# Four moves at the seam between gating and attention: earlier gated weights, a filler behind the second logits, a fixed order up to the last minimum, exchanged transpose banks

## The chip, the core and the metric

The kernel runs on one core of a Trainium2 chip. The core has engines that run side by side: TensorE (PE in the profile; PEld is its loading of weights) multiplies matrices and transposes, VectorE (DVE) and ScalarE (ACT) read and write both memories on the chip, GpSimd (POOL) works on SBUF only, and SyncE (SP) issues most transfers. TensorE writes to PSUM, eight banks of 512 float32 per partition; SBUF holds the tiles. The metric is the time of one execution on the device in microseconds, the median of several runs.

## The reference

One decoder block on 1024 tokens of width 1024, float32. Eight heads of forgetting attention stand beside a gated branch (gMLP); both go through one output projection, and a gated feed-forward with a causal convolution follows. What matters here:

```
proj = rmsnorm(x) @ w_in                      # q, k, v, u, vg, forget gates
att  = softmax(q k^T / 8 + c_q - c_k, causal) @ v     # 8 heads of 64; c: cumulated log forget gates
mixed = tril(w_s[g]) @ rmsnorm(gelu(vg))[chunk, g] + b_s   # 8 groups, chunks of 128 tokens
sg   = gelu(u) * mixed
h    = x + concat(att, sg) @ w_out
h    = h + conv_ffn(rmsnorm(h))
out  = rmsnorm(h)
```

## The kernel before

Every float32 operand of a matmul is split in a high part (float32r, a rounded copy) and a low part (what is left), and a product is three matmuls: high by high, high by low, low by high. A split is a cast (ACT or POOL) and a subtraction (VectorE or POOL), the second in L166 or L787.

The work comes in stages: the input projections (up to 183 us in the trace), the rest of the v projection (`vmul`, L861, four products of 48 matmuls in sums and differences of halves), the spatial gating (`spatial`, L805 to L815), the transposes of the gated result (`turn_sg`, L831), the attention, then the output projection, the feed-forward and the last norm.

The spatial gating goes over eight groups. For each, TensorE mixes both halves of the tokens into one bank; VectorE forms the gated first half, ACT adds the bias to the second half and POOL multiplies it (L815). `turn_sg(hf, c, ps)` then transposes half `hf` (512 tokens) of column block `c`, four 128x128 transposes into one bank; `sg_hi` (ACT) and `sg_lo` (VectorE) split it into `sgT[c]`. Half 0 uses the banks of tag "s", half 1 those of tag "b".

The gated half of the output projection is not a stage of its own. It is cut into sixteen pieces, the fillers (`sg_out`): each is 12 matmuls for 128 tokens by 512 columns (L1068 to L1070), is evacuated by VectorE, which adds the input x (L1071, tile raw, loaded in L1064), and is stored (L1072). The table `FILLS` says behind which step of the attention a filler is issued; (-1, j) means behind the logits of block j of head 0. A filler's bank has the tag "b", of which there are four, shared with the turns and the value products. Its weights are `whs`: two transfers of 512 KB (`sg_load`, L775, tile raw) and four splits (`sg_split`) into buffers of the tag whl, of which there are four too; the last users before them are the weights of the v products.

The attention of a head takes its eight blocks of 128 queries from the longest (7) to the shortest (0). `logits_mm` (L980, L981) needs one of two places of two banks; `logits_min` (VectorE, L993) adds the mask, takes the row's minimum and moves the logits to SBUF, which frees the place; `logits_exp` (ACT, L1003) follows. Then `turn_p` (L1028) transposes the exponentials, cast and subtraction (L1029, L1030) split them, and `values` (L1044) multiplies by v. The attention's PSUM layout lies over that of the stage before: the first two places cover the four banks of tag "s".

What sets the order: the planner of the language puts each engine's instructions in order, by their place in the program and by its own estimate of when they are ready. `after` adds an order between two instructions without a wait. `seq` chains TensorE's instructions from the v products on as written. While `act.on` and `dve.on` are set, all instructions of ACT and VectorE are chained as written; in the trace their line is then L55. They are set from behind `head_loads(0)` up to the second last part of the gate (`sg_lo(1, 3)`), ahead of the first filler. POOL is not chained. SP issues its transfers one by one; one that must wait holds those behind it. `head_loads(h)` (L878 to L886) loads a head's queries, keys and row sums; the row sums of all heads go through memory (ncr, ncd: L850, L903, L910).

Of the kernel before, what the change touches and what calls it, by code (L numbers as in the profile page):

```python
# [12 lines left out]
ALU = mybir.AluOpType  # L13
AX = mybir.AxisListType
P = 128
# [3 lines left out]
NFF = 22  # L19
WARM = 8  # L20

FILLS = {(-1, j): 1 for j in (5, 3, 2)} | {(h, s): 1 for h in range(6) for s in ((0, 2, 4) if h == 0 else (2, 4))}
FCFG = ("b", 4, 4)


# [38 lines left out]
def after(tc, later, earlier):  # L64
    tc.add_manual_dep(later.ins, earlier.ins.name, mybir.DependencyInfo(
        mybir.DependencyClass.NoSync, mybir.DependencyReason.DATA), reason="order")
# [3 lines left out]
def block_kernel(ctx: ExitStack, tc: tile.TileContext, xT, xtok, wuv, wv0, wva, wvk, wvl, wqk, cpk, bfv,  # L70
# [86 lines left out]
    def split_w(src, hl, hi_eng="act", lo_eng="dve"):  # L157
        h, l = hl
        if hi_eng == "act":
            act.copy(h, src)  # L160
        elif hi_eng == "pool":
            pool.tensor_copy(h, src)
        else:
            dve.tensor_copy(h, src)
        eng = dve if lo_eng == "dve" else pool
        return eng.tensor_tensor(out=l, in0=src, in1=f32(h), op=ALU.subtract)  # L166
# [600 lines left out]

    queued = []

    def sg_load(hf):  # L770

        wrs = []
        for kp in range(2):
            wr = sb("raw", [P, 2, 512])
            queued[:] = [sp.dma_start(out=wr, in_=wos[hf, kp])]  # L775
            after(tc, queued[0], loads[0])
            wrs += [wr[:, 0, :], wr[:, 1, :]]
        return wrs

    splits = []  # L780

    def sg_split(wr, hi="act"):
        w = sb("whl", [P, 2, 512], F32R)
        if hi == "pool":
            x = pool.tensor_copy(w[:, 0], wr)
            after(tc, x, splits[0])
            pool.tensor_tensor(out=w[:, 1], in0=wr, in1=f32(w[:, 0]), op=ALU.subtract)  # L787
        else:
            split_w(wr, (w[:, 0], w[:, 1]), hi, "pool")
        return w  # L790

    def spatial_weights():
# [6 lines left out]
    def spatial():  # L799

        tmp = [sb("pt", [P, 4, 256]) for _ in range(2)]
        for g in range(8):
            ps = bank()
            for hf in range(2):
                m = pe.matmul(ps[:, hf * 256:hf * 256 + 256], ws[:, g, :], vgt[hf][:, :, g * 64:(g + 1) * 64],  # L805
                              start=(hf == 0), stop=(hf == 1), skip_group_check=True)
            v3 = lambda t: t.rearrange("p (t d) -> p t d", d=64)
            u = [ut[hf][:, :, g * 64:(g + 1) * 64] for hf in range(2)]
            dve.scalar_tensor_tensor(out=u[0], in0=v3(ps[:, 0:256]), scalar=bs[:, g:g + 1], in1=u[0],
                                     op0=ALU.add, op1=ALU.mult)  # L810
            t = tmp[g // 4][:, g % 4, :]

            def second():
                act.activation(t, ps[:, 256:512], AF.Identity, bias=bs[:, g:g + 1])
                splits[:] = [pool.tensor_tensor(out=u[1], in0=v3(t), in1=u[1], op=ALU.mult)]  # L815

            if g < 7:
                second()
            if g < 2:
                vlow.append(evac_v(6 + g, 0, vb_[:, (2 + g) * 256:(2 + g) * 256 + 256]))  # L820
            if 1 <= g < 5:
                vlow[g - 1]()
        seq(m)
        return second

    def turn_sg(hf, c, ps):

        if hf == 0:
            sgT[c] = sb("G", [P, 2, 1024], F32R)
        for t in range(4):  # L830
            seq(pe.transpose(ps[:, t * P:(t + 1) * P], ut[hf][:, t, c * P:(c + 1) * P], ident))  # L831
        return ps
# [4 lines left out]
    def sg_hi(hf, c, ps):  # L837
        act.copy(sgT[c][:, 0, sg_o(hf)], ps)
# [35 lines left out]
    def head_loads(h):  # L874
# [11 lines left out]
            loads[h] = sp.dma_start(out=f32(b2s[64:67, hh, :]), in_=ncd[1:4, 1 + h, :])  # L886
        rows[h] = sml.tile([P, 8], F32, tag="rs", name=nm("rs"))

    head_loads(0)
    va_, vb_, vc_ = xy[:, 0], xy[:, 1], xl  # L890
    act.on = dve.on = True
# [6 lines left out]
    vmul(R, vw["S1"], "T1")  # L898
    Q = [sbank() for _ in range(2)]
    vmul(Q, vw["A22"], "T4")  # L900
    whs, wrs = [], sg_load(0)
    for n, s in ((0, 1), (1, 1), (2, 2), (3, 1)):
        after(tc, sp.dma_start(out=ncd[n].rearrange("h (t p) -> (h t) p", p=P), in_=sums[s]), queued[0])  # L903
    for j, o in enumerate(hw):
        dve.tensor_tensor(out=vb_[:, o], in0=R[j], in1=vb_[:, o], op=ALU.subtract)
        dve.tensor_tensor(out=vc_[:, o], in0=va_[:, o], in1=R[j], op=ALU.subtract)
    for m in range(4):
        evac_v(m, 0, vk[:, m, :])()
    sp.dma_start(out=vu[1], in_=vc_.rearrange("p (m c) -> p m c", c=256))
# [1 line left out]
    sp.dma_start(out=f32(b2s[64:67, 0, :]), in_=ncd[1:4, 1, :])  # L911
    V.extend(sb("V", [P, 2, 8, 2, 64], F32R) for _ in range(2))
    vlow = [evac_v(4 + m, 0, vb_[:, m * 256:m * 256 + 256]) for m in range(2)]
    for j, o in enumerate(hw):
        dve.tensor_tensor(out=va_[:, o], in0=va_[:, o], in1=Q[j], op=ALU.add)
    sp.dma_start(out=vu[0], in_=va_.rearrange("p (m c) -> p m c", c=256))
# [1 line left out]
    second = spatial()  # L918
    head_loads(1)

    for c in range(4):
        ps = turn_sg(0, c, sbank())
        sg_hi(0, c, ps)
        sg_lo(0, c, ps)
        if c == 0:
            second()
    for k in range(4):
        whs.append(sg_split(wrs[k], "pool" if k < 2 else "act"))


    attT = [None] * 4
# [124 lines left out]
    def sg_out(whs):  # L1056
        for hf in range(2):
            o = slice(hf * 512, hf * 512 + 512)
            for tt in range(8):
                if hf == 0 and tt == 6:  # L1060
                    nxt = sg_load(1)
                ts_ = slice(tt * P, (tt + 1) * P)
                hs = sb("raw", [P, 512])
                sp.dma_start(out=hs, in_=xtok[ts_, o])  # L1064
                ps = fbank()
                for k in range(4):
                    w = whs[k]
                    seq(pe.matmul(ps, sgT[k][:, 0, ts_], w[:, 0, :], start=(k == 0), stop=False))  # L1068
                    seq(pe.matmul(ps, sgT[k][:, 0, ts_], w[:, 1, :], start=False, stop=False))
                    seq(pe.matmul(ps, sgT[k][:, 1, ts_], w[:, 0, :], start=False, stop=(k == 3)))  # L1070
                dve.tensor_tensor(out=hs, in0=ps, in1=hs, op=ALU.add)  # L1071
                sp.dma_start(out=hpd[tt, :, o], in_=hs)  # L1072
                if hf == 0 and tt == 7:
                    whs = [sg_split(wr) for wr in nxt]
                yield

    filler = sg_out(whs)

    wo = []
# [28 lines left out]
        logits_mm(0, j, firsts[j])  # L1108
    for c in range(4):
        sg_hi(1, c, pts[c])  # L1110
    m7 = logits_min(0, 7, firsts[7])
    sg_lo(1, 0, pts[0])
    sg_lo(1, 1, pts[1])
    m6 = logits_min(0, 6, firsts[6])
    sg_lo(1, 2, pts[2])
    logits_exp(0, 7, m7)
    logits_exp(0, 6, m6)
    logits(0, 5)
    sg_lo(1, 3, pts[3])
    act.on = dve.on = False  # L1120
    act.last = dve.last = None
    fill((-1, 5))
    for j in range(4, -1, -1):
        logits(0, j)
        fill((-1, j))
    due = []
    turned = [turn_p(g) for g in STEPS[0]]
    for n, step in enumerate(STEPS):
# [674 lines left out]
```

## Time and profile before

| | |
|---|---|
| median of 3 runs | 1052.77 us (1052.22 to 1052.96) |
| profiled execution | 1052.88 us |
| its span | 1051.2 us |
| TensorE busy | 1040.2 us, 99% |
| VectorE, ACT, POOL busy | 891.5, 562.6, 217.0 us |
| chain that ended last | PE 96%, DVE 2%, ACT 1% |

All times inside the kernel are microseconds from the start of the span of this one execution. In a row of the timeline stand start, length, engine, line, operation, the tile written and the tiles read by the program's names, shapes and a count; in square brackets how long the engine stood idle before it and what ended that. A row with a count merges several instructions.

### The profile page before, as it was taken

To read this page: it belongs to the slowest core of one execution; us is meant where nothing else is said; L and a number is where in the kernel's file an instruction comes from. 1 tells how busy PE (TensorE), PEld (TensorE's weight loads), DVE (VectorE), ACT (ScalarE), POOL (GpSimd) and SP (SyncE) were. 2 spreads that over 40 slices of the span, in tenths; PEclk is the share of its full clock that TensorE was granted. 3 is DMA by queue.
4 is the path that set the end of the run, shared out by engine and by line. 5 is a ranking of instruction groups with operands and counts; after the bars stand their busy time and mean duration, and the time that the engine had idled before them with its cause. 6 is when DMAs were issued, how large, how long until landed. Compare 5 with 4: busy or idle time off the path is not lost.

```text
span 1051.2 us, 14265 instructions
## 1 busy us (share of the span) xinstructions
PE 1040.2 (99%) x4998; PEld 870.1 (83%) x4998; DVE 891.5 (85%) x1302; ACT 562.6 (54%) x1003; POOL 217.0 (21%) x165
## 2 busy tenths in 40 slices
PE   9999999999999999999999999999999999999997
PEld 7988888978888888888888888888888888888886
DVE  6899887868887779998999999898897866997774
ACT  6776632457876746654344344444444554454654
POOL 0000231320421640243333423323331000000000
PEclk9999999999999999999999999999999999999999
DMA  9722558867755544222255332431322899433432
GB/s 326 235 87 95 154 157 244 227 195 199 209 161 161 158 158 156 80 90 91 80 181 171 120 110 82 131 120 67 129 85 81 305 325 305 117 100 98 142 121 100
DMA packets 67451, 161.66 MB, mean 154 GB/s; under 512 B 8094, under 2 KB 9238, under 8 KB 67380
## 3 DMA queue, kind: packets, MB, share of 16 engines
q1 hardware_dynamic: 67108, 160.72, 47.8%
q8 instruction: 39, 0.64, 0.2%
q14 instruction: 32, 0.26, 0.1%
q10 hardware_dynamic: 272, 0.04, 0.0%
HBM read 115.68 MB, written 45.05 MB: 153 GB/s over the span
## 4 chain that ended last, share of the span: by engine, by line
PE 96%; DVE 2%; ACT 1%; issue 0%; ACTq 0%; DVEq 0%
PE k L1616 20%; PE qc L1356 11%; PE qa L1356 11%; PE qd L1356 11%; PE qb L1356 5%; PE pb L270 5%; PE ps L270 5%; PE pb L1044 3%; PE pb L1028 2%; PE qc L510 2%; PE qd L510 2%; PE qa L510 2%; PE ps L861 2%; PE pl L980 1%; PE pf L1068 1%; PE pl L981 1%
## 5 line engine op out<-in xcount | busy, mean ns | idle before, releaser
L1616 PE MATMUL k<-whb,wha 128*128 128x512 f32 (+1 forms) x936 | 209.9, 386 | 0.0
L1616 PEld LDWEIGHTS k<-whb,wha 128*128 128x128 f32 x936 | 174.1, 188 | 35.8 <-DVE wha L166 0.2
L1356 PE MATMUL qc<-xT,whb 128*128 128x512 f32 x540 | 129.9, 389 | 0.2 <-ACT whb L160 0.2
L1356 PE MATMUL qa<-xB,wha 128*128 128x512 f32 x528 | 127.4, 390 | 0.0
L1356 PEld LDWEIGHTS qc<-xT,whb 128*128 128x128 f32 x540 | 101.3, 188 | 21.6 <-ACT whb L160 0.5
L1356 PEld LDWEIGHTS qa<-xB,wha 128*128 128x128 f32 x528 | 98.8, 188 | 20.8 <-DVE wha L166 0.4
L160 ACT CAST wha<-sg 128x512 fp32r<-128x512 f32 x77 | 47.7, 622 | 96.9 <-PE k L1616 83.5
L160 ACT CAST whb<-sg 128x512 fp32r<-128x512 f32 x82 | 50.5, 617 | 87.0 <-PE qc L1356 67.0
L166 DVE TENSOR_TENSOR wha<-sg,wha 128x512 fp32r<-128x512 f32 x77 | 52.7, 687 | 37.1 <-ACT wha L160 36.9
L1356 PE MATMUL qd<-xB,whb 128*128 128x512 f32 x264 | 63.7, 389 | 0.0
L1356 PE MATMUL qd<-xT,whb 128*128 128x512 f32 x264 | 63.7, 389 | 0.0
L1029 ACT CAST pt<-pb 128x512 fp32r<-128x512 f32 x72 | 40.6, 584 | 38.2 <-PE pb L1028 32.0
L1356 PE MATMUL qb<-xT,whb 128*128 128x512 f32 x252 | 61.0, 389 | 0.0
L166 DVE TENSOR_TENSOR whb<-sg,whb 128x512 fp32r<-128x512 f32 x82 | 57.0, 697 | 4.4 <-ACT whb L160 4.3
L1240 POOL TENSOR_TENSOR sg<-raw 128x512 f32<-128x512 f32 x20 | 30.8, 1541 | 141.1 <-DVE whb L166 80.6
L1356 PEld LDWEIGHTS qd<-xT,whb 128*128 128x128 f32 x264 | 49.5, 188 | 10.5 <-DVE u L1463 0.3
L1356 PEld LDWEIGHTS qd<-xB,whb 128*128 128x128 f32 x264 | 49.5, 188 | 10.3
L1030 DVE TENSOR_TENSOR pt<-pb,pt 128x512 fp32r<-128x512 f32 x72 | 47.3, 685 | 12.2 <-ACT pt L1029 11.9
L1356 PEld LDWEIGHTS qb<-xT,whb 128*128 128x128 f32 x252 | 47.2, 188 | 10.0 <-DVE whb L166 0.3
L1044 PE MATMUL pb<-pt,V 128*128 128x512 f32 (+3 forms) x192 | 49.7, 363 | 0.3 <-DVE pt L1030 0.3
L1243 POOL TENSOR_TENSOR sg<-sg,raw 128x512 f32<-128x512 f32 x20 | 33.0, 1649 | 63.1 <-DVE whb L166 63.1
L1241 POOL TENSOR_TENSOR sg<-sg,raw 128x512 f32<-128x512 f32 x20 | 35.1, 1757 | 47.2 <-issue 44.6
(416 smaller groups left out, 2242.6 us busy)
## 6 DMA issues: line engine op xcount, KB each, us to landing
raw<-wup SPq DMA_DIRECT2D x44, 512.0 KB
sg<-hx SPq DMA_DIRECT2D x77, 256.0 KB
hx<-hs SPq DMA_DIRECT2D x44, 256.0 KB
hx<-ca SPq DMA_DIRECT2D x35, 256.0 KB
xT<-wdn SPq DMA_DIRECT2D x28, 256.0 KB
x<-kd SPq DMA_DIRECT2D x24, 256.0 KB
A<-xtok SPq DMA_DIRECT2D x8, 512.0 KB
raw<-wqk SPq DMA_DIRECT2D x8, 512.0 KB
```

Source lines behind the costliest of these rows:

```text
L160: act.copy(h, src)
L166: return eng.tensor_tensor(out=l, in0=src, in1=f32(h), op=ALU.subtract)
L270: pe.matmul(banks[m], xs(n, xi, k)[:, ms], w[:, wi, :], start=(first and k == 0 and c == 0 and (own or m % 2 == 0)), stop=(k == 3 and c == ...
L510: pe.matmul(ps, w[:, wi, ks], xs(n, xi, k), start=(first and c == 0), stop=(c == 11), skip_group_check=True)
L1029: casts.append(act.copy(pt[:, 0, :], ptr))
L1030: los.append(dve.tensor_tensor(out=pt[:, 1, :], in0=ptr, in1=f32(pt[:, 0, :]), op=ALU.subtract))
L1044: seq(pe.matmul(po[half][:, o:o + w], lhs, pt[:, s, c:c + w], start=(new and s == 0), stop=(s == 1 and (half, k) in ((1, 6), (0, 3))), ski ...
L1240: pool.tensor_tensor(out=s[0], in0=a21, in1=a22, op=ALU.add)
L1241: pool.tensor_tensor(out=s[1], in0=s[0], in1=a11, op=ALU.add)
L1243: pool.tensor_tensor(out=s[3], in0=s[1], in1=a12, op=ALU.add)
L1356: pe.matmul(ps, w[:, wi, ks], xb[:, xi, k, :], start=(first and n == 0), stop=(n == 11), skip_group_check=True)
L1616: pe.matmul((banks[bk + m] if ps is None else ps)[:, o], xh[:, xi, ms], wh[:, wi, o], start=((first and p_ == 0 or new) and n == 0), stop= ...
```

## The change

Four things are edited, all between the v products and the turns of head 0.

1. The gated weights of columns 0 to 511 are loaded ahead of `head_loads(0)` on SP, behind the last store of the projections, and split ahead of the spatial gating: the first two wholly on POOL, the last two with the cast on ACT (inside its fixed order) and the subtraction on POOL. The stores of the row sums are put in order behind the head loads instead of behind the weights.
2. The banks of the transposes of half 0 are allocated together, and the last two allocated are used first.
3. The three fillers among the logits of head 0 stand behind blocks 6, 4 and 2 instead of 5, 3 and 2. The first low part of half 1 moves ahead of the minimum of block 7, since a filler needs a bank.
4. ACT and VectorE stay in the written order up to the minimum and exponential of block 0. A filler's evacuation and store is put off in a list while that holds, and taken from it at written places: the first ahead of the exponential of block 5, the others behind their fillers.

```diff
-FILLS = {(-1, j): 1 for j in (5, 3, 2)} | {(h, s): 1 for h in range(6) for s in ((0, 2, 4) if h == 0 else (2, 4))}
+FILLS = {(-1, j): 1 for j in (6, 4, 2)} | {(h, s): 1 for h in range(6) for s in ((0, 2, 4) if h == 0 else (2, 4))}
...
-    def sg_load(hf):
+    def sg_load(hf, floor=None):
...
-            after(tc, queued[0], loads[0])
+            after(tc, queued[0], floor or loads[0])
...
     def sg_split(wr, hi="act"):
         w = sb("whl", [P, 2, 512], F32R)
-        if hi == "pool":
-            x = pool.tensor_copy(w[:, 0], wr)
-            after(tc, x, splits[0])
-            pool.tensor_tensor(out=w[:, 1], in0=wr, in1=f32(w[:, 0]), op=ALU.subtract)
-        else:
-            split_w(wr, (w[:, 0], w[:, 1]), hi, "pool")
+        split_w(wr, (w[:, 0], w[:, 1]), hi, "pool")
         return w
...
+    whs, wrs = [], sg_load(0, floors["sp"])
     head_loads(0)
...
     vmul(Q, vw["A22"], "T4")
-    whs, wrs = [], sg_load(0)
     for n, s in ((0, 1), (1, 1), (2, 2), (3, 1)):
-        after(tc, sp.dma_start(out=ncd[n].rearrange("h (t p) -> (h t) p", p=P), in_=sums[s]), queued[0])
+        after(tc, sp.dma_start(out=ncd[n].rearrange("h (t p) -> (h t) p", p=P), in_=sums[s]), loads[0])
     for j, o in enumerate(hw):
         dve.tensor_tensor(out=vb_[:, o], in0=R[j], in1=vb_[:, o], op=ALU.subtract)
         dve.tensor_tensor(out=vc_[:, o], in0=va_[:, o], in1=R[j], op=ALU.subtract)
+    for k in range(2):
+        whs.append(sg_split(wrs[k], "pool"))
...
     vlow = [evac_v(4 + m, 0, vb_[:, m * 256:m * 256 + 256]) for m in range(2)]
+    for k in range(2, 4):
+        whs.append(sg_split(wrs[k]))
...
+    pts = [sbank() for _ in range(4)]
+    pts = pts[2:] + pts[:2]
     for c in range(4):
-        ps = turn_sg(0, c, sbank())
+        ps = turn_sg(0, c, pts[c])
         sg_hi(0, c, ps)
         sg_lo(0, c, ps)
         if c == 0:
             second()
-    for k in range(4):
-        whs.append(sg_split(wrs[k], "pool" if k < 2 else "act"))
...
-                dve.tensor_tensor(out=hs, in0=ps, in1=hs, op=ALU.add)
-                sp.dma_start(out=hpd[tt, :, o], in_=hs)
+                def evac(ps=ps, hs=hs, tt=tt, o=o):
+                    dve.tensor_tensor(out=hs, in0=ps, in1=hs, op=ALU.add)
+                    sp.dma_start(out=hpd[tt, :, o], in_=hs)
+
+                if dve.on:
+                    EVAC.append(evac)
+                else:
+                    evac()
...
+    sg_lo(1, 0, pts[0])
     m7 = logits_min(0, 7, firsts[7])
-    sg_lo(1, 0, pts[0])
+    fill((-1, 6))
     sg_lo(1, 1, pts[1])
     m6 = logits_min(0, 6, firsts[6])
     sg_lo(1, 2, pts[2])
     logits_exp(0, 7, m7)
     logits_exp(0, 6, m6)
-    logits(0, 5)
+    m5 = logits_min(0, 5, logits_mm(0, 5, place()))
     sg_lo(1, 3, pts[3])
-    act.on = dve.on = False
-    act.last = dve.last = None
-    fill((-1, 5))
+    EVAC.pop(0)()
+    logits_exp(0, 5, m5)
     for j in range(4, -1, -1):
         logits(0, j)
         fill((-1, j))
+        if EVAC:
+            EVAC.pop(0)()
+    act.on = dve.on = False
+    act.last = dve.last = None
```

More of the change, by code (lines that the diff above doesn't have):

```diff
@@ L775, in sg_load @@
             queued[:] = [sp.dma_start(out=wr, in_=wos[hf, kp])]
-            after(tc, queued[0], loads[0])
+            after(tc, queued[0], floor or loads[0])
             wrs += [wr[:, 0, :], wr[:, 1, :]]
         return wrs
-    splits = []
     def sg_split(wr, hi="act"):
         w = sb("whl", [P, 2, 512], F32R)
-        if hi == "pool":
-            x = pool.tensor_copy(w[:, 0], wr)
-            after(tc, x, splits[0])
-            pool.tensor_tensor(out=w[:, 1], in0=wr, in1=f32(w[:, 0]), op=ALU.subtract)
-        else:
-            split_w(wr, (w[:, 0], w[:, 1]), hi, "pool")
+        split_w(wr, (w[:, 0], w[:, 1]), hi, "pool")
         return w
@@ L814, in second @@
                 act.activation(t, ps[:, 256:512], AF.Identity, bias=bs[:, g:g + 1])
-                splits[:] = [pool.tensor_tensor(out=u[1], in0=v3(t), in1=u[1], op=ALU.mult)]
+                pool.tensor_tensor(out=u[1], in0=v3(t), in1=u[1], op=ALU.mult)
             if g < 7:
@@ L1075, in sg_out @@
                 yield
+    EVAC = []
     filler = sg_out(whs)
```

## Prediction

> **What bounds the kernel now.** I read the page first, then busy time by stretch, then the timeline of each engine around the edited lines.
>
> ```profile
> span 1051.2 us, 14265 instructions
> PE 1040.2 (99%) x4998; PEld 870.1 (83%) x4998; DVE 891.5 (85%) x1302; ACT 562.6 (54%) x1003; POOL 217.0 (21%) x165
> ...
> 207.00:228.00 21.00, 18.87 (x108) 15.64 (x107) 14.27 (x29) 13.76 (x32) 8.35 (x10) 1.00 0.57 163
> 228.00:400.00 172.00, 170.39 (x968) 146.06 (x966) 139.86 (x265) 114.03 (x250) 49.66 (x46) 1.00 0.61 179
> ```
>
> In the last two rows the columns are stretch, its length, busy PE, PEld, DVE, ACT and POOL (instructions in brackets), granted clock, DMA share, GB/s. TensorE sets the end almost everywhere; a change pays only where TensorE stands still. From 207 to 228 us, the stretch that the diff rewrites, it is busy 18.87 of 21 us: 2.13 us idle, the largest hole in the attention. Four rows hold it:
>
> ```profile
> 208.78 1.91 PE L831 MATMUL pb<-ident,A 128*128 128x128 f32 x16
> 211.09 0.50 PE L980 MATMUL pl<-x 128*128 128x512 f32 x1 [0.39 <-DVE G L55]
> 213.86 0.50 PE L980 MATMUL pl<-x 128*128 128x512 f32 x1 [0.74 <-DVE mn L55]
> 214.67 0.39 PE L1068 MATMUL pf<-whl,G 128*128 128x512 f32 x1
> ...
> 217.40 0.39 PE L980 MATMUL pl<-x 128*128 128x512 f32 x1
> ...
> 226.16 0.66 PE L1028 MATMUL pb<-ident,t 128*128 128x128 f32 x4 [0.72 <-DVE raw L1071]
> 227.08 1.25 PE L1028 MATMUL pb<-ident,t 128*128 128x128 f32 x8 [0.27 <-DVE raw L1071]
> 228.28 0.73 PE L1044 MATMUL pb<-pt,V 128*128 128x512 f32 x2
> ```
>
> The reader is to see: the first logits (block 7) wait 0.39 us, after the transposes end at 210.69, for a low part of the gate (G) to leave their PSUM banks; block 5 waits 0.74 us for block 7's minimum (mn); two turns of the exponentials (L1028) wait 0.72 and 0.27 us for a filler's evacuation (raw, L1071). Together 2.12 us. The stretch ends where the first value matmul starts, at 228.28.
>
> The profiled execution took 1052.88 us by its own clock, 1.7 us over its span, and stands 0.11 us above the median 1052.77. A difference under 0.2% (2.1 us) is about what a measurement cannot tell from no change.
>
> **The change part by part.** *Transposes' banks.* The first logits take the PSUM of two of the four gate transposes. Exchanged, those are the two drained first.
>
> ```profile
> 209.15 1.89 DVE L55 TENSOR_TENSOR G<-ps,G 128x512 fp32r<-128x512 f32 x3 [0.16 <-ACT G L55]
> 212.46 1.34 DVE L55 CUSTOM_DVE_ANT_0 t<-pl,t,lim 128x1024 f32<-128x1024 f32 x1 [1.43 <-PE pl L981]
> 213.73 1.28 DVE L55 TENSOR_TENSOR G<-pb,G 128x512 fp32r<-128x512 f32 x2
> 214.93 1.20 DVE L55 CUSTOM_DVE_ANT_0 t<-pl,t,lim 128x896 f32<-128x896 f32 x1
> 216.66 1.07 DVE L55 CUSTOM_DVE_ANT_0 t<-pl,t,lim 128x768 f32<-128x768 f32 x1
> ...
> 218.25 0.94 DVE L993 CUSTOM_DVE_ANT_0 t<-pl,t,lim 128x640 f32<-128x640 f32 x1
> ...
> 225.41 0.69 DVE L1071 TENSOR_TENSOR raw<-pf,raw 128x512 f32<-128x512 f32 x1
> 226.34 1.28 DVE L1071 TENSOR_TENSOR raw<-pf,raw 128x512 f32<-128x512 f32 x2
> 227.54 1.87 DVE L1030 TENSOR_TENSOR pt<-pb,pt 128x512 fp32r<-128x512 f32 x3
> ```
>
> Low parts 1 to 3 run 209.15 to 211.04, 0.63 each, so the second is done by 209.8 and the logits start at 210.69, -0.40. Block 6 needs the last (211.04) and starts near 211.6. Next late would be the transposes themselves.
>
> *First filler behind the second logits.* A filler is 12 matmuls, 214.67 to 217.40, 2.73 us. It now covers block 7's minimum. It needs split weights (next part) and a bank: all four are held by the second transposes, hence the low part moved ahead of the minimum. That part takes 0.64 after 211.04, done 211.7, before block 7's logits end at 212.06 (212.46 less 0.40), so the minimum is not delayed. Block 6 ends at 212.4, then the filler. -0.74.
>
> *Fixed order and deferred evacuations.* Now the three evacuations run at 225.41 to 227.6, behind nearly all minima, and hold three banks. In the new order I lay VectorE out with the rows above (a minimum's row less 0.07 overlap, 0.6 per low part and evacuation): minimum 7 212.06 to 213.3; low part 213.95; minimum 6 215.1; low part 215.7; block 5's logits end at 215.15 + 0.7 + 0.3, so minimum 5 216.1 to 217.1; low part 217.7; evacuation 0 218.3; minimum 4 219.2; evacuation 1 waits for its filler (216.5 + 2.73 + 0.3 = 219.5), 220.1; minima 3 and 2, one step of 0.13 shorter each, 220.9 and 221.5; evacuation 2 waits for 223.0, 223.6; minima 1 and 0, 224.4. Each logits tile needs the minimum two blocks above: block 3 (219.2) that of 5 (217.1), block 2 (219.7) that of 4 (219.2), block 1 (222.7) that of 3 (220.9). None waits; the thinnest margin, 0.5 us, is behind evacuation 0, and past it each microsecond is one of TensorE. Behind each new wait on VectorE (evacuations 1 and 2) stand minima whose logits come after that filler on TensorE anyway. TensorE runs its logits and fillers through to 223.3 (224.8 less 1.13 of waits and some 0.3 of slow first matmuls behind them) and starts the turns there, all four banks empty by 223.6: -0.99. The stores behind the evacuations (L1072) go to SP earlier, in front of nothing that waits.
>
> What is late next is the first turn's cast and subtraction before the first value matmul.
>
> ```profile
> 209.95 1.18 ACT L55 CAST whl<-raw 128x512 fp32r<-128x512 f32 x2
> 210.99 2.09 ACT L55 CAST G<-pb 128x512 fp32r<-128x512 f32 x4
> ...
> 226.04 0.57 ACT L1029 CAST pt<-pb 128x512 fp32r<-128x512 f32 x1
> ```
>
> By TensorE alone (turns from 223.3, 16 transposes at 0.12 by the row of 208.78) the values could start at 225.2. The first cast takes 0.57 and the subtraction 0.65, the latter behind minimum 0 (224.4): done at 225.1 if the cast goes first, 226.6 if it stands behind the last two exponentials. In the row above the cast stands between them; the same here gives 226.0. So the stretch is 2.3 us shorter, between 1.7 and 3.1.
>
> *Gated weights earlier.* Two loads of 512 KB move past the head loads on SP; two POOL casts and two POOL subtractions go ahead of the mixing products, two ACT casts too, with two more POOL subtractions.
>
> ```profile
> 187.58 2.26 SPq L632 DMA_DIRECT2D qd<-G  x2
> ...
> 190.61 0.93 SPq L878 DMA_DIRECT2D x<-qd  x1
> ...
> 194.10 1.00 SPq L775 DMA_DIRECT2D raw<-wos  x2
> ...
> 205.14 0.23 SPq L910 DMA_DIRECT2D x<-ncd  x1
> ...
> 212.29 1.31 SPq L1064 DMA_DIRECT2D raw<-xtok  x3
> 194.00:196.00 2.00, 2.00 (x19) 2.00 (x18) 1.84 (x4) 0.00 (x0) 0.04 (x1) 1.00 0.86 254
> 204.00:206.00 2.00, 2.00 (x11) 1.75 (x10) 2.00 (x5) 0.77 (x3) 1.45 (x2) 1.00 0.17 65
> 193.21 0.29 POOL L851 CAST t<-t 72x128 fp32r<-72x128 f32 x1 [8.38 <-DMA t<-ncr]
> ...
> 202.27 1.60 POOL L815 TENSOR_TENSOR A<-pt,A 128x256 f32<-128x256 f32 x2 [8.22 <-ACT pt L55]
> ...
> 208.72 0.73 POOL L815 TENSOR_TENSOR A<-pt,A 128x256 f32<-128x256 f32 x1 [0.17 <-ACT pt L55]
> 209.39 1.17 POOL L785 CAST whl<-raw 128x512 fp32r<-128x512 f32 x2
> 210.52 2.52 POOL L787 TENSOR_TENSOR whl<-raw,whl 128x512 fp32r<-128x512 f32 x2
> 197.45 0.91 ACT L55 ACTIVATE V<-x,rstd 128x256 fp32r<-128x256 f32 x2 [6.35 <-PE ps L861]
> 201.72 0.47 ACT L55 ACTIVATE pt<-pb,cp 128x256 f32<-128x256 f32 x1 [3.35 <-DVE A L55]
> 194.37 2.80 PE L861 MATMUL ps<-whl,V 128*128 128x256 f32 x22
> ```
>
> The small load ahead (t<-ncr, after the stores at 187.58) is in at 193.2. At 254 GB/s each 512 KB takes 2.1 us, so the weights land at 195.3 and 197.4. The head loads lose 1.00 us of issue and 4.2 us of data; the DMA share falls to 0.17 after 204, so all are in by 204 in either order, and logits want them at 210.7: nothing. The row sums (L910, 205.14) wait for stores behind the same bytes: nothing.
>
> POOL needs 1.17 + 2.52 for the first two: 195.3 to 199.0. ACT is free 198.36 to 201.72. Its first cast (0.59) fits at 198.4; the second writes a buffer that the last V product reads (48 matmuls from 194.37, 0.12 each: 200.1), so 200.2 to 200.8. POOL's other two subtractions, 2.52, end near 202.8, half a microsecond into the product at 202.27. Eight products at 0.73 take 5.8 and end by 208.6, before the last one's own release at 208.72; its transposes come at 210.2. So POOL may be free as late as 204.4: nothing, margin 1.6 us. If that cover is gone, TensorE waits one for one. What it gives back: ACT loses 1.18 us ahead of the second high parts (from 210.99 to about 210.1), in time for the early low part.
>
> A rule speaks against this. The Trainium skill, "GPSIMD Engine Reference", section "1. Specifications", says that POOL shares its SBUF interfaces with VectorE and contends with VectorE instructions that have two SBUF inputs. This trace has both sides: POOL's subtraction takes 1.26 in the row above, and the same size takes 1.76 beside VectorE's weight splits in the row below. With all four at 1.76 POOL would be free at 204.8 and the sum would be 0.4 us smaller; I keep 1.26, since VectorE mostly reads PSUM in this stretch.
>
> ```profile
> L1241 POOL TENSOR_TENSOR sg<-sg,raw 128x512 f32<-128x512 f32 x20 | 35.1, 1757 | 47.2 <-issue 44.6 <-DVE whb L166 1.8 <-POOL sg L1240 0.7
> ```
>
> The fillers' input loads (L1064) land within the DMA burst after 212.29, by 218; evacuation 0 wants its own at 217.7.
>
> **Sum.** 1052.88 - 2.3 = 1050.6; TensorE is busy 170.39 of 172 us behind the stretch, so what is won stays won. Ends: -3.1 gives 1049.8, -1.7 gives 1051.2.
>
> **The rivals.** *The turns take the wait over.* If the planner puts casts behind both exponentials and the subtraction behind the minima, or evacuation 0 is late for its input, half of the gain goes: two first waits, 1.14 us, stay gone, 1051.7. For: VectorE is laid full from 212 to 224; against: the row 226.04.
>
> *The weights come too late, POOL becomes the bound (slower).* If SP keeps the head loads (1.5 MB, 6.1 us) in front, the weights land at 201.4 and 203.5. POOL's first splits end at 205.1, ACT's casts stand in the fixed order ahead of its part of the mixing until 204.7, POOL ends at 207.6 and the products at 213.4: TensorE waits 3.2 us at the last transposes, and 5.2 if POOL subtracts at 1.76. Against the gain of 2.3 that is 1053.8 to 1055.8. It decides from the first landing: no loss to 196.9, even at 199.2, slower by 0.2% from 201.3. Against: only a late store stands in front of the loads in the new order.
>
> *The planner's order elsewhere shifts.* Later VectorE and ACT orders are the planner's; the other waits of the attention sum to 170.39 against 172, so 1.6 us at most can be won, and as much lost.
>
> **How the numbers follow.** The likeliest case 0.57 (1049.8 to 1051.2, predicted 1050.5 with the small store effects); turns take over 0.20 (1051.7); POOL bound 0.13 (1053.8 to 1055.8); shifts elsewhere 0.10 (1049 to 1054.5). Faster by over 0.2% means under 1050.7: two thirds of the first and a third of the last, and a little of the second for its spread, 0.45. Slower means over 1054.9: half of the POOL case, but its size is bounded from few rows, and the last, 0.16 with that allowance. Within: 0.39. Range 1049.1 to 1054.2.
>
> **What would show it.** Right: no wait at the first logits; a filler's matmul before block 5's logits; evacuations between minima; turns near 223; POOL's weight splits done by 203; value matmuls at 225 to 226.6. Wrong: a wait before the second transposes (POOL or ACT), a wait of logits on minimum 4, or POOL products ending after 210.

## The result and the profile after

The changed kernel takes 1050.33 us (median of 11 runs, 1049.76 to 1051.8), the kernel before 1052.62 us beside it (11 runs, 1051.99 to 1055.91). The ratio is 0.9976, with a 95% interval of 0.9967 to 0.9986: faster by about a quarter of a per cent. Predicted were 1050.5 us.

The profiled execution of the changed kernel took 1051.8 us, the longest of its 11. Its page:

```profile
span 1050.1 us, 14270 instructions
PE 1038.9 (99%) x4998; PEld 870.7 (83%) x4998; DVE 891.3 (85%) x1302; ACT 563.4 (54%) x1003; POOL 218.8 (21%) x165
```

Its busy time by stretch (columns as in the prediction), and behind it one row of the same view of the kernel before, for the time ahead of anything edited:

```profile
207.00:226.00 19.00, 18.46 (x105) 15.81 (x104) 14.74 (x29) 11.21 (x24) 4.07 (x6) 1.00 0.79 253
0.00:190.00 190.00, 187.31 (x927) 157.82 (x928) 161.47 (x251) 111.28 (x202) 21.73 (x23) 1.00 0.57 184
```

```profile
0.00:190.00 190.00, 188.71 (x938) 158.76 (x939) 163.01 (x253) 111.61 (x205) 21.53 (x23) 1.00 0.59 185
```

From 207 to 226 us TensorE is idle 0.54 us, where 2.13 were idle from 207 to 228. It stood still 2.69 us before 190 us in this execution against 1.29 in that of before, 1.40 more, and everything behind is as much later. All of it lies in the first 10 us, which the diff does not touch. Times below are therefore lengths, not positions: "the stretch" is from the first of the transposes of half 1 (pb<-ident,A) to the first value matmul of head 0 (pb<-pt,V). Before it is 208.78 to 228.28, 19.50 us. The timeline of TensorE in the changed kernel:

```profile
210.15 2.21 PE L824 MATMUL pb<-ident,A 128*128 128x128 f32 x16
212.82 0.50 PE L977 MATMUL pl<-x 128*128 128x512 f32 x1 [0.45 <-DVE G L55]
...
225.50 1.94 PE L1025 MATMUL pb<-ident,t 128*128 128x128 f32 x16
227.52 0.73 PE L1041 MATMUL pb<-pt,V 128*128 128x512 f32 x2
```

The stretch is 17.37 us, 2.13 shorter. The waits on block 7's minimum and on the fillers' evacuations are gone: all sixteen transposes of the first turns go through in one piece of 1.94 us, and the values follow at once. The wait of the first logits for the low part G is still there, 0.45 us. The same kernel was run once more (experiment 10); its timeline in the same view:

```profile
208.64 1.91 PE L824 MATMUL pb<-ident,A 128*128 128x128 f32 x16
210.94 0.50 PE L977 MATMUL pl<-x 128*128 128x512 f32 x1 [0.39 <-DVE G L55]
...
223.62 1.94 PE L1025 MATMUL pb<-ident,t 128*128 128x128 f32 x16
225.64 0.74 PE L1041 MATMUL pb<-pt,V 128*128 128x512 f32 x2
```

Here the stretch is 17.00 us, 2.50 shorter than before, and the execution took 1049.94 us. Two parts make up the 2.50. Up to the turns it is 14.98 us (208.64 to 223.62) against 16.03 (208.78 to 224.81, the first turn's start before): 1.05. From there to the values it is 2.02 against 3.47: 1.45. Each is larger than the idle time recorded in it (0.74, and 0.72 + 0.27 = 0.99), by 0.31 and 0.46. TensorE's rows overlap in the profile as long as it goes on without a break (a matmul's row of 0.40 us is followed by the next 0.23 us after its start); at a wait the overlap with the row ahead is lost, and the first matmul behind it takes 0.50 us instead of 0.39. A wait costs more than its bracket says.

VectorE and ACT in this second execution (experiment 10):

```profile
218.04 0.68 DVE L55 TENSOR_TENSOR raw<-pf,raw 128x512 f32<-128x512 f32 x1
...
219.85 0.69 DVE L55 TENSOR_TENSOR raw<-pf,raw 128x512 f32<-128x512 f32 x1 [0.27 <-PE pf L1067]
...
223.46 0.69 DVE L55 TENSOR_TENSOR raw<-pf,raw 128x512 f32<-128x512 f32 x1 [1.59 <-issue]
...
224.28 0.59 ACT L1026 CAST pt<-pb 128x512 fp32r<-128x512 f32 x1 [1.56 <-PE pb L1025]
224.76 0.51 ACT L55 ACTIVATE gg<-gg,mn 128x256 f32<-128x256 f32 x1
```

The evacuations now stand between the minima. The last starts 0.16 us before the turns (223.46 against 223.62), and no turn waits for its bank. The first cast of the turns goes ahead of the last two exponentials (224.28 against 224.76); before, it stood between them.

### The profile page after: what moved, and what is told of

The parts are those of the page before. It is cut to its first block, busy times and chain, and to the rows that moved or that the text cites. A ratio compares the mean times of both kernels' runs of the same rounds, so it can differ in the third digit from the quotient of the medians.

```text
span 1050.1 us, 14270 instructions
## 1 busy us (share of the span) xinstructions
PE 1038.9 (99%) x4998; PEld 870.7 (83%) x4998; DVE 891.3 (85%) x1302; ACT 563.4 (54%) x1003; POOL 218.8 (21%) x165
## 4 chain that ended last, share of the span: by engine, by line
PE 91%; DVE 3%; DMA 3%; ACT 2%; issue 1%; SPq 0%; POOL 0%; ACTq 0%; POOLq 0%; DVEq 0%
PE k L1624 20%; PE qc L1364 11%; PE qa L1364 11%; PE qd L1364 11%; PE qb L1364 5%; PE pb L270 5%; PE ps L270 5%; PE pb L1041 2%; PE pb L1025 2%; PE qc L510 2%; PE qd L510 2%; PE qa L510 2%; PE pl L977 1%; PE pl L978 1%; PE pf L1065 1%; PE pf L1067 1%
```

## The experiments

Where an experiment says "one time", the kernel was executed once; where an interval is given, there were five rounds. With all of them the kernel before ran on the same chip: once beside experiments 1 to 4 (1052.44 us), 11 or 15 times beside the others, where its median is given. The lengths of the stretch are steadier than the times of whole executions (17.00 to 17.03 us in experiments 1 and 6 to 10, whose profiled executions took 1049.89 to 1052.15), so parts are compared by the stretch.

**1. Without the exchange of banks.** Of the changed kernel only this line is taken out:

```diff
     pts = [sbank() for _ in range(4)]
-    pts = pts[2:] + pts[:2]
```

> Measure: from the start of the second transposes to the first value matmul, 19.50 us in the kernel before (208.78 to 228.28) and 17.37 us in the changed one (210.15 to 227.52). This is the changed kernel without the exchange of the transposes' banks. Theory as predicted (the exchange puts the first logits on the banks that are drained first, and something else took that gain): without it the first logits wait for the last low part, a wait of 0.45 us or more stays or grows, 17.4 to 17.9 us. Rival (allocating the four banks together already turns their order, and the exchange turns it back to what it was before): without it the wait of the first logits on a low part of the gate is gone and the stretch is 0.4 us shorter, 16.9 to 17.0 us.

```profile
208.71 1.91 PE L824 MATMUL pb<-ident,A 128*128 128x128 f32 x16
209.07 1.89 DVE L55 TENSOR_TENSOR G<-ps,G 128x512 fp32r<-128x512 f32 x3 [0.16 <-ACT G L55]
211.01 0.50 PE L976 MATMUL pl<-x 128*128 128x512 f32 x1 [0.39 <-DVE G L55]
...
225.73 0.74 PE L1040 MATMUL pb<-pt,V 128*128 128x512 f32 x2
```

The stretch is 17.02 us, the wait 0.39, one time 1050.0 us against 1052.44. With and without the line the same (17.00 and 0.39 in experiment 10): neither expectation had it so, and the rival's 16.9 to 17.0 us came close by luck, since the wait that it had gone is there. The row of VectorE shows what is waited for: the low parts of columns 1 to 3 end at 210.96, and the logits start 0.05 us later. In the compiled programs, as experiment 12 put on record, the columns 0, 1, 2, 3 of the first transposes lie in banks 2, 0, 3, 1 in all three kernels, before, changed and this one, and the first logits cover banks 0 and 1; the column that is drained last, 3, stays under them. So the line exchanges names only. It fits that a bank is given out when a tile is first written, in the order of writing; no run tested that by itself.

**2. The weights late.** The changed kernel with loads and splits where they were before (and the stores of the row sums in their old order):

```diff
-    whs, wrs = [], sg_load(0, floors["sp"])
     head_loads(0)
...
     vmul(Q, vw["A22"], "T4")
+    whs, wrs = [], sg_load(0)
...
-    for k in range(2):
-        whs.append(sg_split(wrs[k], "pool"))
...
-    for k in range(2, 4):
-        whs.append(sg_split(wrs[k]))
...
+    for k in range(4):
+        whs.append(sg_split(wrs[k], "pool" if k < 2 else "act"))
```

> The changed kernel with the gated weights loaded and split where they were before (behind the head loads and behind the mixing products). Theory (the early weights only make the early filler possible): the first filler now waits for POOL's splits, which ended at 215.5 us in the kernel before where the filler wants them from 212.4 on; 1.1 us of waits among the filler's matmuls, less the 0.3 us that the early splits cost in the transposes; 18.0 to 18.6 us. Rival (the weights' place does not matter here): 17.0 to 17.4 us, no wait at the filler.

```profile
215.13 0.50 PE L1071 MATMUL pf<-whl,G 128*128 128x512 f32 x1 [0.20 <-POOL whl L166]
```

The stretch is 17.51 us, one time 1050.08 against 1052.44. The first filler runs up to its last group of weights, then waits 0.20 us for POOL's last subtraction. Half a microsecond (17.51 less 17.00) is all that the early weights buy, less than expected: even in their old place the splits end only a little too late for the filler's new place.

**3. The early weights alone.** The kernel before, with only the loads and splits moved ahead (the lines of experiment 2 the other way round).

> The kernel before with the gated weights loaded and split early, nothing else changed. Theory (the weights alone win nothing, since the filler did not wait for them, and POOL's later products cost 0.3 us in the second transposes): 19.5 to 19.9 us against 19.50 before, all four waits still there. Rival (freeing ACT and POOL from the splits is where the gain comes from): under 18.6 us.

The stretch is 19.55 us against 19.50, with all four waits in it; one time 1053.39 against 1052.44. Alone the move wins nothing, as the theory had it: it serves the filler's new place, and there only with the half microsecond of experiment 2.

**4. Fillers in their old places.** The changed kernel, fixed order kept; with no early filler, the first evacuation goes behind the logits of block 4:

```diff
-FILLS = {(-1, j): 1 for j in (6, 4, 2)} | ...
+FILLS = {(-1, j): 1 for j in (5, 3, 2)} | ...
...
-    fill((-1, 6))
     sg_lo(1, 1, pts[1])
...
     m5 = logits_min(0, 5, logits_mm(0, 5, place()))
+    fill((-1, 5))
     sg_lo(1, 3, pts[3])
-    EVAC.pop(0)()
     logits_exp(0, 5, m5)
```

> The changed kernel with the fillers behind blocks 5, 3 and 2 as before, the rest kept. Theory (the first filler covers block 7's minimum): block 5's logits wait for that minimum again, 0.74 us and 0.1 to 0.3 us of slow restart, 18.1 to 18.5 us. Rival (the fixed order with evacuations between the minima carries the whole gain): 17.3 to 17.5 us.

```profile
214.03 0.50 PE L977 MATMUL pl<-x 128*128 128x512 f32 x1 [0.75 <-DVE mn L55]
```

The stretch is 18.09 us, one time 1051.33 against 1052.44. Block 5 waits 0.75 us for block 7's minimum, as it did before. The place is worth 1.1 us (18.09 less 17.00), by the wait, the slower start behind it and the overlap lost at it.

**5. The order freed early.** The changed kernel, with the fixed order ended behind the first evacuation instead of behind the last minimum:

```diff
     EVAC.pop(0)()
     logits_exp(0, 5, m5)
+    act.on = dve.on = False
+    act.last = dve.last = None
     for j in range(4, -1, -1):
...
-    act.on = dve.on = False
-    act.last = dve.last = None
```

> The changed kernel with the fixed order of ACT and VectorE given up behind the first evacuation, as early as before, so that the second and third evacuations stand where the planner puts them. Measure as before: from the start of the second transposes to the first value matmul, 19.50 us before and 17.37 us changed. Theory (the late evacuations held the banks that the turns wait for): two of the three evacuations come behind the last minima again and the turns wait for them, 0.3 to 1.0 us, 17.7 to 18.5 us. Rival (one evacuation early is enough, or the planner finds the order by itself): 17.3 to 17.5 us and no wait at the turns.

VectorE's last minimum and its first evacuation, then TensorE:

```profile
223.87 0.41 DVE L990 CUSTOM_DVE_ANT_0 gg<-pl,t,lim 128x128 f32<-128x128 f32 x1
224.20 0.69 DVE L55 TENSOR_TENSOR raw<-pf,raw 128x512 f32<-128x512 f32 x1
...
224.94 0.66 PE L1025 MATMUL pb<-ident,t 128*128 128x128 f32 x4 [1.05 <-DVE raw L55]
225.82 1.25 PE L1025 MATMUL pb<-ident,t 128*128 128x128 f32 x8 [0.22 <-DVE raw L1069]
227.10 0.70 PE L1041 MATMUL pb<-pt,V 128*128 128x512 f32 x2
```

The stretch is 18.84 us (from 208.26), one time 1051.45 against 1052.88. The turns wait again, 1.05 and 0.22 us. Even the evacuation that is written ahead of the freed part (L55 in its row) runs behind all minima: nothing chained any longer keeps the minima behind it, and the planner puts them first. The fixed order is worth 1.8 us in the changed kernel, more than expected. Together with the 1.1 of experiment 4 and the 0.5 of experiment 2 that is 3.4 us, more than the 2.5 won, so the single worths do not add. Most of the excess can be accounted for, though no run held it apart: the 0.5 is a part of the 1.1, since without early weights the filler's new place wins that much less; and from the turns to the values this run takes 3.84 us, 0.37 more than the 3.47 of the kernel before, so it is worse than the order that was replaced.

**6. Half of the splits behind the products.** The changed kernel; the split of the second weight and the fourth weight's subtraction go behind POOL's products again (`splits[0]` is the last of these products):

```diff
...
-    for k in range(2):
-        whs.append(sg_split(wrs[k], "pool"))
+    whs = [sg_split(wrs[0], "pool"), None, None, None]
...
-    for k in range(2, 4):
-        whs.append(sg_split(wrs[k]))
+    whs[2] = sg_split(wrs[2])
+    whs[3] = sb("whl", [P, 2, 512], F32R)
+    act.copy(whs[3][:, 0], wrs[3])
...
+    whs[1] = sb("whl", [P, 2, 512], F32R)
+    x = pool.tensor_copy(whs[1][:, 0], wrs[1])
+    after(tc, x, splits[0])
+    for k in (1, 3):
+        x = pool.tensor_tensor(out=whs[k][:, 1], in0=wrs[k], in1=f32(whs[k][:, 0]), op=ALU.subtract)
+        after(tc, x, splits[0])
```

> The changed kernel with half of POOL's split work (one cast and one subtraction of weight 1, the subtraction of weight 3) put behind the mixing products. Theory (POOL, free about 0.6 us too late for the first product, sends its products, ACT's bias steps and the high parts back by 0.3 to 0.4 us): POOL is free before the first product, the second transposes take 1.9 us instead of 2.2 and the stretch is 0.3 us shorter, 17.0 to 17.1 us, the wait of the first logits still there. Rival (the transposes are slow for another reason): 17.3 to 17.4 us.

The stretch is 17.03 us, one time 1049.89 against 1052.88. POOL's products start as early as before the change (6.52 us ahead of the transposes of half 1), and nothing is won by it against the 17.00 and 17.02 of experiments 10 and 1. What POOL's lateness costs is seen only where the weights land late; POOL's rows of experiment 10 and, with one of ACT, of the profiled execution of the changed kernel, in this order:

```profile
196.06 1.66 POOL L162 CAST whl<-raw 128x512 fp32r<-128x512 f32 x2 [2.18 <-DMA raw<-wos]
202.83 3.52 POOL L808 TENSOR_TENSOR A<-pt,A 128x256 f32<-128x256 f32 x4
206.94 2.81 POOL L808 TENSOR_TENSOR A<-pt,A 128x256 f32<-128x256 f32 x4 [0.58 <-ACT pt L55]
```

```profile
198.36 1.47 POOL L162 CAST whl<-raw 128x512 fp32r<-128x512 f32 x2 [3.05 <-DMA raw<-wos]
204.75 3.53 POOL L808 TENSOR_TENSOR A<-pt,A 128x256 f32<-128x256 f32 x4
208.31 1.21 ACT L55 ACTIVATE pt<-pb,cp 128x256 f32<-128x256 f32 x3 [1.46 <-POOL A L808]
208.86 2.79 POOL L808 TENSOR_TENSOR A<-pt,A 128x256 f32<-128x256 f32 x4 [0.58 <-ACT pt L55]
```

Measured from the first transpose of half 1, the weights are in 12.58 us ahead in the first and 11.79 in the second; the products start 5.81 and 5.40 ahead, and the last ends 1.11 and 1.50 behind it. In the second the transposes took 2.21 instead of 1.91 us and the stretch 17.37 instead of 17.00. The first four products take 0.88 us each, not 0.73, and ACT's fifth bias step waits for the fourth of them (1.46 us, the ACT row), so that POOL's lateness passes through ACT to the last products. That the later landing made the whole difference of 0.37 is argued from these rows; no run held it apart.

**7. Both.** Experiment 6 without the exchange line, to see whether the two margins add.

> Half of POOL's split work behind the mixing products and no exchange of banks, both on the changed kernel. Theory: the two leftovers add, 0.3 us of transposes and 0.45 us of wait, stretch 16.5 to 16.8 us, and the kernel is 0.7 us faster than the changed one, near 1049.6 us. Rival (VectorE or the first turn's cast becomes the limit): the stretch stays at 17.0 us or more with a wait at the first value matmul.

1050.01 us (median of 7, 1049.58 to 1051.33) against 1052.88, ratio 0.9973 (0.9962 to 0.9984); the stretch is 17.01 and the wait 0.39. The time is the changed kernel's and the wait is there: the two margins add to nothing.

**8. An exchange by other tiles.** If new tiles get their bank on writing, tiles that exist already keep theirs; so those of a v product were taken:

```diff
-    pts = [sbank() for _ in range(4)]
-    pts = pts[2:] + pts[:2]
+    pts = [Q[0], Q[1], sbank(), sbank()]
```

> The changed kernel, where the transposes of columns 0 and 1 are written into the two tiles of the last v product themselves, so that they take those banks whatever the planner hands out; columns 2 and 3 take the two other banks. Stretch as before: 17.37 us in the changed kernel, 17.02 without the exchange. Theory (the planner hands a bank to the tile that is written first, whatever the order of allocation, so that the exchange in the change moved nothing; the first logits wait for whatever stands in the last product's banks): the logits start directly behind the transposes, 0.4 us sooner (1.9 instead of 2.3 us behind the transposes' start), stretch 16.6 us, or 16.9 if POOL is late again. Rival (the first logits wait for all four low parts, whichever banks they are in): the wait stays, 17.0 to 17.4 us.

The stretch is 17.01 us and the wait 0.39; one time 1051.48 against 1052.4, with a late head as in the profiled execution above. The columns now lie in banks 3, 1, 2, 0 (on record with experiment 12): the last one is again in a bank that the first logits cover.

**9. Experiments 6 and 8 together.**

> As the last, and half of POOL's split work behind the mixing products. Theory: both leftovers gone, stretch 16.6 us, kernel 0.4 to 0.8 us under the changed one, 1049.5 to 1049.9 us. Rival (first wait stays): stretch 17.0 us, 1049.9 to 1050.3 us.

1050.8 us (median of 11, 1049.62 to 1052.15) against 1052.4, ratio 0.9981 (0.9972 to 0.999); the stretch is 17.02. Nothing is gained on the changed kernel, as the rival had it.

**10. The changed kernel again.**

> The changed kernel itself once more. Theory (whether POOL's splits end in time depends on when the weights land, which differs by half a microsecond between executions, and the exchange has no part in it): if the weights land 12.2 us or more ahead of the second transposes, as without the exchange, these run without a break and the stretch is 17.0 us. Rival (the exchange costs it): 17.3 to 17.4 us again although the weights land as early.

The stretch of 17.00 us shown above, with the weights 12.58 us ahead, as the theory had it; one time 1049.94 against 1052.4. That is 2.5 us less than the median beside it, as much as the stretch lost. Against the one profiled execution of the kernel before, the span is 3.0 us shorter (1048.2 and 1051.2): 2.50 in the stretch, 0.14 ahead of it, and about 0.35 behind it, where no line is edited. The same 0.35 shows in the first profiled execution of the changed kernel; its cause stays open, and there is only one trace of the kernel before.

**11. The loads late, the splits early.** The slower rival of the prediction made real: the changed kernel with the two loads behind the head loads on SP, the splits still ahead of the gating.

```diff
-    whs, wrs = [], sg_load(0, floors["sp"])
     head_loads(0)
+    whs, wrs = [], sg_load(0)
...
-        after(tc, sp.dma_start(out=ncd[n].rearrange("h (t p) -> (h t) p", p=P), in_=sums[s]), loads[0])
+        after(tc, sp.dma_start(out=ncd[n].rearrange("h (t p) -> (h t) p", p=P), in_=sums[s]), queued[0])
```

> The changed kernel with the gated weights loaded behind the head loads again, but split ahead of the mixing products as changed: the slower rival of the prediction made real. Theory: POOL becomes the bound, its last product ends 3 to 5 us later and the second transposes or the logits behind them wait; stretch plus what TensorE loses in the mixing products together 2.5 to 5 us more than in the changed kernel, time 1052.5 to 1055 us. Rival (POOL has more slack than worked out): under 1 us more, under 1051.5 us.

One time 1056.26 us against 1052.4. The timeline of POOL, ACT and TensorE:

```profile
203.10 1.36 POOL L162 CAST whl<-raw 128x512 fp32r<-128x512 f32 x2 [9.31 <-DMA raw<-wos]
204.32 1.14 ACT L55 CAST whl<-raw 128x512 fp32r<-128x512 f32 x2 [6.18 <-DMA raw<-wos]
205.88 3.72 PE L798 MATMUL pb<-G,pt 128*128 128x256 f32 x16 [2.36 <-ACT pt L55]
209.71 5.53 POOL L808 TENSOR_TENSOR A<-pt,A 128x256 f32<-128x256 f32 x8
211.19 0.64 PE L824 MATMUL pb<-ident,A 128*128 128x128 f32 x4
212.55 0.65 PE L824 MATMUL pb<-ident,A 128*128 128x128 f32 x4 [0.72 <-POOL A L808]
...
232.04 0.73 PE L1041 MATMUL pb<-pt,V 128*128 128x512 f32 x2
```

POOL waits 9.31 us for the weights and ACT 6.18, since its casts stand in the fixed order ahead of its bias steps. TensorE pays twice: 2.36 us in the mixing products, which wait for ACT, then some 0.72 us at each further column of the transposes, which wait for POOL's products at the pace of two per 1.38. The stretch is 20.85 us, 3.85 longer than in experiment 10; with the 2.36 ahead of it that is 6.2 of the 6.32 us between the two executions (1056.26 and 1049.94). The mechanism is the one expected; the loss is larger, for two reasons. ACT's hold was priced in the prediction for POOL's path alone, not as a stop of TensorE. And TensorE lost clock, so that the eight matmuls of the first two logits took 3.09 us instead of 1.85, 1.24 of the 3.85 (busy time by stretch; the column behind POOL's is the granted clock):

```profile
203.00:206.00 3.00, 0.64 (x4) 0.24 (x3) 1.38 (x3) 1.68 (x4) 2.90 (x4) 1.00 0.42 163
212.00:215.00 3.00, 1.31 (x8) 0.84 (x8) 2.03 (x4) 1.95 (x4) 3.00 (x5) 1.00 1.03 221
215.00:217.00 2.00, 1.71 (x6) 1.56 (x7) 0.00 (x0) 0.78 (x2) 0.23 (x1) 0.59 1.03 301
217.00:219.00 2.00, 2.00 (x7) 1.58 (x6) 0.75 (x1) 0.01 (x1) 0.00 (x0) 0.56 1.05 404
219.00:222.00 3.00, 3.00 (x15) 2.51 (x14) 2.93 (x6) 1.88 (x3) 0.00 (x0) 1.00 0.54 209
```

**12. The first logits over the columns drained first.** The changed kernel, with the four tiles of the v products taken in the order that puts columns 0, 1, 2, 3 into banks 1, 0, 3, 2 (read from the compiled program):

```diff
-    pts = [sbank() for _ in range(4)]
-    pts = pts[2:] + pts[:2]
+    pts = [Q[1], R[1], Q[0], R[0]]
```

> The placement in the built kernels says that the first logits take banks 0 and 1, and that columns 0 to 3 are transposed into banks 2, 0, 3, 1 in the kernel before, in the changed kernel and without the exchange alike, and into 3, 1, 2, 0 where the last product's tiles were reused: column 3, drained last, is under the first logits in all of them. Here columns 0 to 3 go into banks 1, 0, 3, 2, by writing them into four tiles of the v products; the rest is the changed kernel. Theory (the first logits wait for the last drained of banks 0 and 1): they start directly behind the transposes, 1.9 instead of 2.3 us behind the second transposes' start, and the stretch is 16.6 us against 17.0, unless the weights land late (then 0.3 more); near 1049.8 us. Rival (they wait for all four low parts): 2.3 and 17.0 us.

```profile
208.12 1.91 PE L824 MATMUL pb<-ident,A 128*128 128x128 f32 x16
209.78 0.48 PE L976 MATMUL pl<-x 128*128 128x512 f32 x1
...
222.46 1.94 PE L1024 MATMUL pb<-ident,t 128*128 128x128 f32 x16
224.48 0.74 PE L1040 MATMUL pb<-pt,V 128*128 128x512 f32 x2
```

The first logits start 1.66 us behind the first transpose, without a wait, against 2.30 in experiment 10: 0.64 sooner for a recorded wait of 0.39; the other 0.25 is the overlap with the last transposes, which run until 210.03. The stretch is 16.36 us. All of it reaches the values, so the minima, which VectorE now starts earlier too, do not become late next. Measured are 1049.57 us (median of 11, 1048.78 to 1050.71) against 1052.89, ratio 0.9971 (0.9962 to 0.998). That is the lowest time of the study and faster than before. On the changed kernel the gain is shown by the stretch (0.64 us); the intervals of the two ratios overlap, so the times alone do not show it.

## Why the prediction was right, and where it was wrong

- **The sum.** 2.3 us were predicted for the stretch, 2.50 measured in experiment 10 and 2.13 in the profiled execution. The time, 1050.33 us, is 2.3 below the 1052.62 beside it. The mechanisms of the fillers and of the fixed order were right; that the size fits as well as this is luck, since two misses cancel, next.
- **The exchange of banks (-0.40): wrong.** The step that failed is "exchanged, those are the two drained first". I took the order of the tiles in the list for the order of the banks; experiment 1 shows that the line moves nothing, and the wait stayed at 0.39 to 0.45. Experiment 12 shows that the mechanism was right: with the banks really exchanged it is worth 0.64. The rival that the change does not do what it says should have been drawn up for this part alone.
- **The first value matmul (2.7 us behind the turns): too late.** I let the first cast stand between the last two exponentials, as in the row of before. It went ahead of both, the subtraction started right behind the last minimum (224.90) and ended at 225.59, almost with the last turn (225.56), and the values came at 225.64, 2.02 us behind the turns. The 0.68 gained here against the forecast pays for the wait that stayed.
- **Turns at 223.3.** 14.52 us behind the first transpose by the prediction, 14.98 measured. The first logits' wait stayed, which is 0.64 by experiment 12; the two waits together had been priced 0.18 too low (1.51 by the prediction; 16.03 less the 14.34 of experiment 12 is 1.69).
- **The filler behind the second logits (-0.74): right, undersized.** No wait on the minimum is left; experiment 4 prices the place at 1.1.
- **Fixed order and evacuations (-0.99): right, undersized.** From the turns to the values 1.45 were won; experiment 5 prices the order at 1.8 in the changed kernel. The laid-out order held: evacuations 9.40, 11.21 and 14.82 us behind the first transpose in experiment 10 against 8.9, 10.7 and 14.2 predicted (217.7, 219.5 and 223.0 less 208.78), each later by 0.5 or 0.6, about what the wait of the first logits cost, and no logits wait on the minimum that stands behind evacuation 0.
- **The early weights (nothing, margin 1.6 us): the cost was right, the margin was not.** The first cast came at 196.06 in experiment 10 instead of 195.3, and four products took 0.88 us each. POOL was free for its products at 202.83, as forecast, yet they ended 1.11 us behind the first transpose of half 1, where those of the kernel before ended 0.67 behind it (209.45 and 208.78), and 0.2 us ahead of the transposes that read the last of them (209.95, twelve of sixteen behind 208.64). In the profiled execution, 0.41 us later relative to it, the stretch was already 0.37 longer. So the margin is a few tenths. The step that failed is "eight products at 0.73 ... may be free as late as 204.4": it took the duration from the row of a single product and left out that ACT's bias steps wait for POOL's products, so that POOL cannot catch up.
- **The rule against it.** The Trainium skill, "GPSIMD Engine Reference", section "1. Specifications", has POOL contend with VectorE for SBUF interfaces. The four subtractions took 1.25 to 1.30 us each (4.99 and 5.19 us in rows of four), not 1.76, so the trace is on the side of the value kept. A sign of contention stands on VectorE's side: four of its steps that read V and wy took 2.37 us together in experiment 10 (at 195.62), where POOL's first casts ran beside them, and 1.66 and 1.67 in the kernel before and in experiment 2, where POOL stood still. The products' 0.88 against 0.73 may be the same, which no run held apart.
- **The slower rival: right in kind.** Experiment 11 gives one time of 1056.26, above the 1053.8 to 1055.8 predicted.
- **The signs named ahead.** In experiment 10 the turns (223.62), the first value matmul (225.64) and the end of the weight splits (202.88) came as said, and POOL's products ended at 209.75, just inside the limit of 210. The wait at the first logits, which was to be gone, was there.

## What to carry to other kernels

Look up in the compiled program which bank or buffer a tile got before an order of tiles is counted as an order of banks; a list exchanged in the source may exchange nothing. Price a wait of TensorE at more than its bracket (here 0.64 for 0.39, 1.1 for 0.74), since the overlap of neighbouring matmuls is lost at it, and in the second case the first matmul behind it is slower too. When work moves ahead of a chain that two engines hand back and forth, its margin is not the slack of the last handover alone: take durations from the contended place, and count that a late engine delays the one that feeds it.

## What the runs showed of the hardware that was not expected

TensorE's clock fell in experiment 11 without one long gap. The longest wait in its trace was 2.36 us; it was busy 0.64 of 3 us at 203 to 206 and 1.31 of 3 us at 212 to 215, at full clock, and then got 0.59 and 0.56 from 215 to 219 while it had work; from 219 on it was 1.00 again. The slow matmuls took 0.63 us instead of 0.40. The Trainium skill, "TensorE: Matmul & The Clock Gate", section "Part 1: The HAM clock gate", ties the lower clock to an idle window of about 3.4 us, and under "A second HAM failure mode: psum-queue depth-cycling" has it come from frequent short idle times as well. This trace agrees with the second: broken activity was enough. How much idle time decides was not measured.

The head of the kernel varies between executions by over a microsecond although nothing there differs: TensorE's idle time before 190 us was 1.29 in the trace of before, 2.69 in that of the changed kernel and 1.61 when the changed kernel ran again. The 1.40 are more than half of what the whole change is worth, and a reason to compare parts by the length of a stretch rather than by the time of one execution.
